# A third Strassen stage in the down projection of a feed-forward block

## Chip, cores and metric

The kernel runs on one core of one Trainium2 chip. The metric is the time of one execution in microseconds (us) as the device reports it; the median of several runs is given. A profiled execution has a time of its own, and its trace has a span, which is a little shorter.

## What is computed

A streaming encoder of two layers on one sequence of 512 tokens, width 1024, in float32. Each layer has a feed-forward block, a mixer (attention and a convolution) and a second feed-forward block:

```python
D_MODEL, SEQ, DEPTH, D_FF = 1024, 512, 2, 2816

def swiglu(x, w_gate, w_up, w_down):
    return (jax.nn.silu(x @ w_gate) * (x @ w_up)) @ w_down

for l in range(DEPTH):
    x = x + 0.5 * swiglu(rms_norm(x, ffn1_norm[l]), ffn1_w_gate[l], ffn1_w_up[l], ffn1_w_down[l])
    ...                                   # mixer: x = x + concat(attn, conv) @ w_out[l]
    x = x + 0.5 * swiglu(rms_norm(x, ffn2_norm[l]), ffn2_w_gate[l], ffn2_w_up[l], ffn2_w_down[l])
    x = rms_norm(x, post_norm[l])
```

So there are four feed-forward blocks. The change concerns their last matrix product, `@ w_down`, from 2816 to 1024.

## The kernel before

**Layout.** Everything is kept transposed: `x` is a tile of 128 partitions x 8 x 512 (8 slices of 128 features, 512 tokens along the free dimension). A product of float32 precision is made of three TensorE matmuls (`mm3`, lines 154 to 156): each operand is split into a high part, a rounded copy made by ScalarE (ACT), and a low part, the rest, made by VectorE (DVE); high x high, high x low and low x high are added in PSUM. Every weight tile therefore costs a load, a cast on ACT (L138 or L244) and a subtraction on DVE (L144 or L246) before TensorE can use it. For some weights the low part is made by a negated copy on ACT (L389) and an accumulating DMA issued by GpSimd (POOL, L390).

**A feed-forward block.** The 2816 hidden features are 22 tiles of 128, in 11 pairs. `CHUNKS` groups the pairs: 0-1, 2-4, 5-7, 8-10. Pairs 0 and 1 use plain products. Pairs 2 to 10 (`pair`) compute gate and up of 256 features with seven products in place of eight (the Strassen-Winograd scheme), from sums of weight quarters that DVE makes (L408 to L411) and from operands that were prepared while pairs 0 and 1 ran. A pair loads its quarters into the buffers `fr` (4 of them) and `raw` (3). Its result is one of two things. `quartered` pairs leave the sums that a Strassen down stage needs (`b11`, `b21`, `b22`, `t1` to `t4`; L445 to L452 and three splits, L161 and L162). The others leave two plain split tiles.

**The down projection.** After pairs 0-1 and after pairs 8-10 it is a *full* one: for each of the 8 slices of the output, `group` runs `mm3` with 512 columns over all hidden tiles of the chunk (4, or 6), then `x` gets its update (L589) and `done(m)` is called. After pairs 2-4 and 5-7 it is a *Strassen stage* (`down`): for each half `g` of the output, seven products of 3 pairs x 2 x 3 matmuls with 256 columns, with sums of weight quarters on DVE (L489, L491, L492, L496) and seven updates of `x` (L480). Both halves' quarters are loaded into the same buffers.

**What follows a block.** `done(m)` prepares slice `m` of the next block's operand: high part on ACT (L167), low part on DVE (L168), a square on ACT and its sum, on POOL for the first slices and on DVE for the last (L191). In layer 0's second block `done2` does so for two sums. In the last block (`Finish`) the last two slices are computed in halves of the tokens (`halved`, L601), then the result is turned and stored.

**Order.** The program is a straight line of instructions; a planner orders each engine's queue by a simulated time line and places the waits. Some orders are forced with `tc.issue_after`: the products of `pair` and `down` follow each other on TensorE by `order["pe"]`. Within an engine the order is fixed when the program runs. Buffers of one tag are used in rotation: the hi and lo weights have 4 each (`wh`, `wl`), `raw` 3.

Of the kernel before, what the change touches and what calls it, by code (L numbers as in the profile page):

```python
# [18 lines left out]
L = 2  # L19
# [17 lines left out]
WIDE = 6  # L37
NP = 3
NC = 2
CHUNKS = ((0, 2), (2, 5), (5, 8), (8, 11))  # L40
CONV = "DAAD"
AHEAD = 2
PAUSE = 16
# [28 lines left out]


@with_exitstack
def encoder_kernel(ctx: ExitStack, tc: tile.TileContext, xT, consts, vecs, rgain, wgu1, wd1, wdq1,
                   wcv, wql, wkl, wuq, wkv, wout, wgu2, wd2, wdq2, out):
    nc = tc.nc
    PSUM = bass.MemoryType.PSUM
    cpool = ctx.enter_context(tc.tile_pool(name="const", bufs=1))
# [7 lines left out]
    def nm(s):  # L87
        uid[0] += 1
        return f"{s}{uid[0]}"
# [44 lines left out]
    def load_w(src, w, kind=""):  # L134
        raw = wpool.tile([P, WC], FP, tag="raw", name=nm("raw"), bufs=3)
        nc.sync.dma_start(out=raw[:, :w], in_=src)
        hi = wpool.tile([P, WC], FR, tag="wh", name=nm("wh"))
        order["cast"] = A.copy(hi[:, :w], raw[:, :w]).ins  # L138
# [5 lines left out]
        (G if kind in POOLW.split() else V).tensor_tensor(lo[:, :w], raw[:, :w], hi[:, :w].bitcast(FP),  # L144
                                                          ALU.subtract)
        return hi, lo

    def low():
        return wpool.tile([P, WC], FR, tag="wl", name=nm("wl"))
# [96 lines left out]
        order["lo"] = V.tensor_tensor(lo[:, :w], src[:, :w], hi[:, :w].bitcast(FP), ALU.subtract).ins  # L246
        return hi, lo

    def ffn(l, gx, norm, wgu, wd, wdq, gain, done, w0=None, halved=KD):
        with tc.tile_pool(name="f", bufs=4) as fpool:  # L250
            ffn_body(fpool, l, gx, norm, wgu, wd, wdq, gain, done, w0, halved)

    def ffn_body(fpool, l, gx, norm, wgu, wd, wdq, gain, done, w0, halved):

# [203 lines left out]
                     "t3": [w[:, h0] for w in us], "t2": [w[:, h1] for w in us],  # L458
                     "t1": [w[:, h0] for w in vs], "t4": [w[:, h1] for w in vs]}]

        def down(act, chunk):

            n = 2 * NP * P
            for g in range(2):
                a11, a12, a21, a22, s3 = quarters(wdq[l, g, chunk], n)
                px, py, pz = bank(), bank(), bank()

                def times(o, src, name, start, q=None, lo=None):
                    hi, lo = split_into(name, src, n) if q is None else summed(wdq[l, g, chunk, q], src, n, lo)
                    with tc.issue_after(order["pe"]):  # L470
                        for k in range(NP):
                            for i in range(2):
                                c = slice((i * NP + k) * P, (i * NP + k + 1) * P)
                                last = mm3(o[:, i * HS:(i + 1) * HS], hi[:, c], lo[:, c], *act[k][name],
                                           start and k == 0 and i == 0, k == NP - 1, True)
                    order["pe"] = last

                def add(row, h, o, sign):
                    v = x[:, 4 * g + 2 * (1 - row):4 * g + 2 * (1 - row) + 2, h * HS:(h + 1) * HS]
                    return V.scalar_tensor_tensor(v, o.rearrange("p (m t) -> p m t", m=2), 0.5 * sign, v, ALU.mult,  # L480
                                                  ALU.add).ins
                times(px, a11, "b11", True)
                with after("u0"):
                    add(0, 0, px, 1)
                times(py, a12, "b21", True, 1)
                with after("u"):
                    add(0, 0, py, 1)
                with after("first") if g else nullcontext():
                    V.tensor_tensor(s3[:, :n], a11[:, :n], a21[:, :n], ALU.add)  # L489
# [7 lines left out]
                lo = subtracted(wdq[l, g, chunk, 3], a22, n)  # L497
# [23 lines left out]

        for p0, p1 in CHUNKS:
            f0, fn = 2 * p0, 2 * (p1 - p0)
            act = []
            last = p1 == NF // 2
            for p in range(p0, p1):
                if p == 0:
                    os = []
                    for r in range(2):
# [18 lines left out]
                elif p < CHUNKS[0][1]:  # L548
                    for r in range(2):
                        ws = [load_w(wgu[l, p, 2 * r + q], WC) for q in range(2)]  # L550
                        o = [bank(), bank()]
                        if w0 and not r:
                            with tc.issue_after(order["mm"]):
                                plain(o[:1], ws, KS[:KD // 4])
                            with tc.issue_after(order["mm"]):
                                R = norm()
                            with after("spread"):
                                plain(o[:1], ws, KS[KD // 4:])
                                plain([None] + o[1:], ws, range(KD))
# [422 lines left out]
    class Finish:  # L982
# [117 lines left out]
    norm = Norm(st)  # L1100
    for l in range(L):
        nx, st1, done = follow(l, "gm")
        ffn(l, gx, norm, wgu1, wd1, wdq1, vv(l, "g1"), done, w0 if l == 0 else None)
        gx = nx
        nx, st2, done = follow(l, "g2")
        mix(l, gx, Norm(st1), done)
# [4 lines left out]
        if l + 1 < L:  # L1111
# [9 lines left out]
            ffn(l, gx, norm2, wgu2, wd2, wdq2, vv(l, "g2"), done2)  # L1121
            gx = nx

            class NormPost(Norm):
# [21 lines left out]
            norm = NormPost(st3)  # L1146
        else:
            end = Finish(st3, gp)
            ffn(l, gx, norm2, wgu2, wd2, wdq2, vv(l, "g2"), end.done, halved=KD - 2)
            end()  # L1150


# [88 lines left out]
```

## Time and profile before

| | |
|---|---|
| median of 3 runs | 1804.32 us (1804.24 to 1805.02) |
| the profiled execution | 1804.94 us, span 1803.1 us, granted TensorE clock 0.998 |
| TensorE matmul (PE) busy | 1781.6 us, 99% |
| TensorE weight load (PEld) busy | 1603.1 us, 89% |
| VectorE (DVE) busy | 1493.0 us, 83% |
| ScalarE (ACT) busy | 1091.9 us, 61% |
| GpSimd (POOL) busy | 420.2 us, 23% |
| DMA | 226.16 MB, mean 125 GB/s |

Engines work side by side and wait for each other by semaphores. PE's matmuls are pipelined, so a busy PE is not PE at its peak: the distance between the starts of two matmuls says more than their duration. "L589" is line 589 of the kernel. A wait is put down to the instruction that ended last before it.

### The profile page before, as it was taken

Reading aid. Unit: us, or ns where it says so; the run is one execution under the profiler, and the core shown is the slowest. Engines: PE = TensorE matmul, PEld = TensorE weight load, DVE = VectorE, ACT = ScalarE, POOL = GpSimd, SP = SyncE. Lnnn points to the kernel's source line nnn. Section 1 sums busy time; section 2 is a strip of 40 time slices with the busy share of each in tenths; the row PEclk is TensorE's granted clock in tenths of the full one; section 3 lists DMA queues with packets and bytes.
Section 4 is the critical chain, followed back from the end, with each engine's and each line's share of the span. In section 5 each row is a group of like instructions: output and inputs, shape, how many; then the busy total and the mean of one; then the engine's idle time right before and its main releaser. Section 6 shows DMA issues by size and latency. Waiting matters only on the chain. (4 is left out here: it accounts for less than half of the span.)

```text
span 1803.1 us, 29267 instructions
## 1 busy us (share of the span) xinstructions
PE 1781.6 (99%) x11334; PEld 1603.1 (89%) x11334; DVE 1493.0 (83%) x2263; ACT 1091.9 (61%) x1721; POOL 420.2 (23%) x343
## 2 busy tenths in 40 slices
PE   9999999999999999999999999999999999999998
PEld 7899999888788899999888999998978788999997
DVE  7898988689956989898779989876998668989884
ACT  5565656457953575756645656554779435656564
POOL 1000010258943000000310000002689410000102
PEclk9999999999999999999999999999999999999999
DMA  5657574325103466665426575743250125575742
GB/s 167 173 127 182 134 174 125 108 88 136 29 24 100 124 167 160 153 159 129 125 63 169 126 191 122 193 110 111 80 151 3 42 83 161 139 183 134 180 119 74
DMA packets 70412, 226.16 MB, mean 125 GB/s; under 512 B 7936, under 2 KB 8320, under 8 KB 70272
## 3 DMA queue, kind: packets, MB, share of 16 engines
q1 hardware_dynamic: 54000, 169.74, 29.7%
q0 software_dynamic: 16128, 54.53, 17.6%
q8 instruction: 89, 1.46, 0.3%
q14 instruction: 51, 0.42, 0.1%
q10 hardware_dynamic: 144, 0.00, 0.0%
HBM read 222.15 MB, written 2.10 MB: 124 GB/s over the span
## 5 line engine op out<-in xcount | busy, mean ns | idle before, releaser
L155 PE MATMUL ps<-r,wh 128*128 128x256 f32 (+1 forms) x2540 | 805.8, 318 | 0.0
L154 PE MATMUL ps<-r,wh 128*128 128x256 f32 (+1 forms) x2540 | 802.9, 320 | 2.3 <-ACT wh L1060 1.5
L156 PE MATMUL ps<-r,wl 128*128 128x256 f32 (+1 forms) x2348 | 750.0, 321 | 1.7 <-DVE wl L246 1.6
L154 PEld LDWEIGHTS ps<-r,wh 128*128 128x128 f32 x2540 | 480.4, 189 | 44.1 <-ACT wh L138 3.7
L155 PEld LDWEIGHTS ps<-r,wh 128*128 128x128 f32 x2540 | 481.4, 190 | 34.2 <-issue 1.4
L156 PEld LDWEIGHTS ps<-r,wl 128*128 128x128 f32 x2348 | 445.0, 190 | 36.7 <-DVE wl L246 3.2
L373 PE MATMUL ps<-xj,wh 128*128 128x512 f32 x864 | 304.8, 392 | 4.6 <-DVE t L426 4.6
L138 ACT CAST wh<-raw 128x1024 fp32r<-128x1024 f32 (+3 forms) x148 | 132.3, 903 | 203.6 <-PE ps L155 100.3
L390 POOL DMA_DIRECT2D ls<-in_wgu x72 | 62.5, 869 | 734.4 <-ACT ls L389 656.5
L244 ACT CAST wh<-fr 128x1024 fp32r<-128x1024 f32 (+1 forms) x160 | 157.8, 986 | 109.7 <-DVE fr L410 51.3
L144 DVE TENSOR_TENSOR wl<-raw,wh 128x1024 fp32r<-128x1024 f32 (+3 forms) x132 | 145.2, 1108 | 84.7 <-ACT wh L138 84.3
L246 DVE TENSOR_TENSOR wl<-fr,wh 128x1024 fp32r<-128x1024 f32 (+1 forms) x160 | 182.1, 1138 | 20.5 <-ACT wh L244 20.5
L373 PEld LDWEIGHTS ps<-xj,wh 128*128 128x128 f32 x864 | 161.3, 188 | 36.3 <-DVE t L426 6.2
L930 POOL TENSOR_TENSOR y<-y,pr 128x511 f32<-128x511 f32 (+14 forms) x120 | 158.1, 1318 | 54.9 <-ACT pr L926 47.5
L374 PE MATMUL ps<-xj,ls 128*128 128x256 f32 x576 | 161.3, 280 | 0.0
L246 DVE TENSOR_TENSOR wl<-raw,wh 128x1024 fp32r<-128x1024 f32 (+1 forms) x100 | 113.4, 1134 | 14.8 <-ACT wh L244 14.4
L244 ACT CAST wh<-raw 128x1024 fp32r<-128x1024 f32 (+1 forms) x100 | 98.1, 981 | 44.7 <-PE ps L155 27.7
L191 POOL TENSOR_TENSOR r<-r,t 128x512 f32<-128x512 f32 x45 | 75.1, 1678 | 175.7 <-ACT t L187 174.9
L374 PEld LDWEIGHTS ps<-xj,ls 128*128 128x128 f32 x576 | 108.3, 188 | 0.2
L389 ACT ACTIVATE ls<-fr 128x1024 fp32r<-128x1024 f32 (+1 forms) x56 | 56.1, 1001 | 85.3 <-PE ps L374 49.5
L926 ACT ACTIVATE pr<-m,vec 128x511 f32<-128x511 f32 (+14 forms) x120 | 85.8, 737 | 12.4 <-POOL y L930 12.4
L922 DVE SCALAR_TENSOR_TENSOR cv<-m,vec,cv 128x511 f32<-128x511 f32 (+14 forms) x120 | 87.8, 732 | 3.6 <-ACT cv L918 2.2
(242 smaller groups left out, 2926.2 us busy)
## 6 DMA issues: line engine op xcount, KB each, us to landing
fr<-in_wgu SPq DMA_DIRECT2D x112, 512.0 KB, 4.2
ls<-in_wgu POOLq DMA_DIRECT2D x72, 512.0 KB, 6.6
raw<-in_wgu SPq DMA_DIRECT2D x62, 512.0 KB, 4.9
fr<-in_wdq SPq DMA_DIRECT2D x48, 384.0 KB, 5.3
ls<-in_wdq POOLq DMA_DIRECT2D x32, 384.0 KB, 4.7
raw<-in_wd SPq DMA_DIRECT2D x32, 384.0 KB, 3.1
raw<-in_wd SPq DMA_DIRECT2D x32, 256.0 KB, 2.7
raw<-in_wcv SPq DMA_DIRECT2D x16, 512.0 KB, 3.6
```

The costliest lines, as they stand in the source:

```text
L138: order["cast"] = A.copy(hi[:, :w], raw[:, :w]).ins
L144: (G if kind in POOLW.split() else V).tensor_tensor(lo[:, :w], raw[:, :w], hi[:, :w].bitcast(FP), ALU.subtract)
L154: T.matmul(o, lh, rh, start=first, stop=False, skip_group_check=free)
L155: T.matmul(o, lh, rl, start=False, stop=False, skip_group_check=free)
L156: order["mm"] = T.matmul(o, ll, rh, start=False, stop=last, skip_group_check=free).ins
L244: A.copy(hi[:, :w], src[:, :w])
L246: order["lo"] = V.tensor_tensor(lo[:, :w], src[:, :w], hi[:, :w].bitcast(FP), ALU.subtract).ins
L373: T.matmul(o, w[0][:, c], both, start=start and k == 0, stop=False, skip_group_check=True)
L374: last = T.matmul(o[:, 0:HS], w[1][:, c], both[:, 0:HS], start=False, stop=k == 3, skip_group_check=True).ins
L922: V.scalar_tensor_tensor(acc[:, s:], u[c][:, :S - s], tap(k), acc[:, s:], ALU.mult, ALU.add)
L926: A.activation(pr[:, s:], u[c][:, :S - s], AF.Copy, scale=tap(k))
L930: order["conv"] = G.tensor_tensor(acc[:, s:], acc[:, s:], pr[:, s:], ALU.add).ins
```

## The change

Pairs 8 and 9 become quartered pairs in a chunk of their own, and a third Strassen stage with 2 pairs (`NR = 2`) takes their down projection. Pair 10 is left alone in the last chunk: its products are issued ahead of that third stage (`held = pair(p1, False)`), and the full down projection now runs over its two hidden tiles only. The weights of this smaller full projection are loaded for four output slices at a time (`load_cols`, twice) in place of once for each slice. The weights of the third stage come in an array of their own (`wdr`). Two sums of squares move: in `Finish` all of those on whole slices from POOL to DVE, in `done2` the second sum for every other slice.

```diff
-CHUNKS = ((0, 2), (2, 5), (5, 8), (8, 11))
+NR = 2
+CHUNKS = ((0, 2), (2, 5), (5, 8), (8, 10), (10, 11))
...
+    def load_cols(wd, l, m, f0, fn):
+
+        raw = wpool.tile([P, WC], FP, tag="raw", name=nm("raw"), bufs=3)
+        nc.sync.dma_start(out=raw.rearrange("p (m f) -> p m f", m=4),
+                          in_=wd[l, m:m + 4, :, f0 * P:(f0 + fn) * P].rearrange("m p f -> p m f"))
+        hi = wpool.tile([P, WC], FR, tag="wh", name=nm("wh"))
+        A.copy(hi, raw)
+        lo = low()
+        V.tensor_tensor(lo, raw, hi.bitcast(FP), ALU.subtract)
+        return hi, lo
+
+    def part_w(ws, m, fn):
+        return [w[:, m % 4 * fn * P:(m % 4 + 1) * fn * P] for w in ws[m // 4]]
...
-        def down(act, chunk):
+        def down(act, quarters_of):
 
-            n = 2 * NP * P
+            np_ = len(act)
+            n = 2 * np_ * P
             for g in range(2):
-                a11, a12, a21, a22, s3 = quarters(wdq[l, g, chunk], n)
+                a11, a12, a21, a22, s3 = quarters(quarters_of(g), n)
...
-                        for k in range(NP):
+                        for k in range(np_):
...
         for p0, p1 in CHUNKS:
             f0, fn = 2 * p0, 2 * (p1 - p0)
-            act = []
             last = p1 == NF // 2
-            for p in range(p0, p1):
+            act = held if last else []
+            for p in range(p0, p1) if not last else ():
...
                 else:
                     order.setdefault("pe", order["mm"])
-                    act += pair(p, p0 > 0 and not last)
+                    act += pair(p, True)
             if p0 and not last:
-                down(act, (p0 - CHUNKS[0][1]) // NP)
+                c = (p0 - CHUNKS[0][1]) // NP
+                if p1 == CHUNKS[-1][0]:
+                    held = pair(p1, False)
+                down(act, lambda g: wdq[l, g, c] if c < NC else wdr[l, g])
                 continue
...
+            if last:
+                wide_w = [load_cols(wd, l, 4 * q, f0, fn) for q in range(2)]
             for m in range(halved if last else KD):
-                if m in ahead:
+                if last:
+                    pd = bank()
+                    group(pd, part_w(wide_w, m, fn), act, range(fn), fn)
+                elif m in ahead:
...
-                ws = [load_w(wd[l, m, :, f0 * P:(f0 + fn) * P], fn * P) for m in ms]
+                ws = [part_w(wide_w, m, fn) for m in ms]
...
-                self.st.add(x[:, m, :])
+                self.st.add(x[:, m, :], eng=V)
...
-                st4.add(x[:, m, :], last=m == KD - 1)
+                st4.add(x[:, m, :], last=m % 2 == 1)
```

More of the change, by code (lines that the diff above doesn't have):

```diff
@@ L74, in encoder_kernel @@
 @with_exitstack
-def encoder_kernel(ctx: ExitStack, tc: tile.TileContext, xT, consts, vecs, rgain, wgu1, wd1, wdq1,
-                   wcv, wql, wkl, wuq, wkv, wout, wgu2, wd2, wdq2, out):
+def encoder_kernel(ctx: ExitStack, tc: tile.TileContext, xT, consts, vecs, rgain, wgu1, wd1, wdq1, wdr1,
+                   wcv, wql, wkl, wuq, wkv, wout, wgu2, wd2, wdq2, wdr2, out):
     nc = tc.nc
@@ L247, in split_into, with ffn, ffn_body @@
         return hi, lo
-    def ffn(l, gx, norm, wgu, wd, wdq, gain, done, w0=None, halved=KD):
+    def ffn(l, gx, norm, wgu, wd, wdq, wdr, gain, done, w0=None, halved=KD):
         with tc.tile_pool(name="f", bufs=4) as fpool:
-            ffn_body(fpool, l, gx, norm, wgu, wd, wdq, gain, done, w0, halved)
-    def ffn_body(fpool, l, gx, norm, wgu, wd, wdq, gain, done, w0, halved):
+            ffn_body(fpool, l, gx, norm, wgu, wd, wdq, wdr, gain, done, w0, halved)
+    def ffn_body(fpool, l, gx, norm, wgu, wd, wdq, wdr, gain, done, w0, halved):
         def quarter():
@@ L459, in pair @@
                      "t1": [w[:, h0] for w in vs], "t4": [w[:, h1] for w in vs]}]
-        def down(act, chunk):
-            n = 2 * NP * P
+        def down(act, quarters_of):
+            np_ = len(act)
+            n = 2 * np_ * P
             for g in range(2):
-                a11, a12, a21, a22, s3 = quarters(wdq[l, g, chunk], n)
+                a11, a12, a21, a22, s3 = quarters(quarters_of(g), n)
                 px, py, pz = bank(), bank(), bank()
                 def times(o, src, name, start, q=None, lo=None):
-                    hi, lo = split_into(name, src, n) if q is None else summed(wdq[l, g, chunk, q], src, n, lo)
+                    hi, lo = split_into(name, src, n) if q is None else summed(quarters_of(g)[q], src, n, lo)
                     with tc.issue_after(order["pe"]):
-                        for k in range(NP):
+                        for k in range(np_):
                             for i in range(2):
-                                c = slice((i * NP + k) * P, (i * NP + k + 1) * P)
+                                c = slice((i * np_ + k) * P, (i * np_ + k + 1) * P)
                                 last = mm3(o[:, i * HS:(i + 1) * HS], hi[:, c], lo[:, c], *act[k][name],
-                                           start and k == 0 and i == 0, k == NP - 1, True)
+                                           start and k == 0 and i == 0, k == np_ - 1, True)
                     order["pe"] = last
@@ L1102, in encoder_kernel @@
         nx, st1, done = follow(l, "gm")
-        ffn(l, gx, norm, wgu1, wd1, wdq1, vv(l, "g1"), done, w0 if l == 0 else None)
+        ffn(l, gx, norm, wgu1, wd1, wdq1, wdr1, vv(l, "g1"), done, w0 if l == 0 else None)
         gx = nx
@@ L1148, in encoder_kernel @@
             end = Finish(st3, gp)
-            ffn(l, gx, norm2, wgu2, wd2, wdq2, vv(l, "g2"), end.done, halved=KD - 2)
+            ffn(l, gx, norm2, wgu2, wd2, wdq2, wdr2, vv(l, "g2"), end.done, halved=KD - 2)
             end()
@@ L1175, in quarters, with down_quarters, down_main, down_rest @@
         return w.transpose(1, 5, 6, 3, 4, 0, 2, 7).reshape(L, NF // 2, 4, P, WC)
-    def down_quarters(w):
-        n0, n1 = CHUNKS[0][1], CHUNKS[-1][0]
-        w = w.reshape(L, NF // 2, 2, P, 2, 2, 2, P)[:, n0:n1, :, :, :, ::-1].reshape(L, NC, NP, 2, P, 2, 2, 2, P)
-        return w.transpose(0, 5, 1, 6, 3, 4, 7, 2, 8).reshape(L, 2, NC, 4, P, 2 * NP * P)
+    def down_quarters(w, n0, nc, np_):
+        w = w.reshape(L, NF // 2, 2, P, 2, 2, 2, P)[:, n0:n0 + nc * np_, :, :, :, ::-1]
+        w = w.reshape(L, nc, np_, 2, P, 2, 2, 2, P)
+        return w.transpose(0, 5, 1, 6, 3, 4, 7, 2, 8).reshape(L, 2, nc, 4, P, 2 * np_ * P)
+    def down_main(w):
+        return down_quarters(w, CHUNKS[0][1], NC, NP)
+    def down_rest(w):
+        return down_quarters(w, CHUNKS[-2][0], 1, NR)[:, :, 0]
     def feat(v):
@@ L1229 @@
         "wgu2": quarters(a["ffn2_w_gate"], a["ffn2_w_up"]), "wd2": cols(a["ffn2_w_down"]),
-        "wdq2": down_quarters(a["ffn2_w_down"]),
+        "wdq2": down_main(a["ffn2_w_down"]), "wdr2": down_rest(a["ffn2_w_down"]),
     }
```

6 lines of the change are left out of this document (3 added, 3 removed).

## The prediction

> **What bounds the kernel now.** I read the page first, then the windows of the feed-forward block that runs from 0 to 350 us, then who waits for whom, then the groups of instructions by shape. The page's first row gives the engines' busy times:
>
> ```profile
> PE 1781.6 (99%) x11334; PEld 1603.1 (89%) x11334; DVE 1493.0 (83%) x2263; ACT 1091.9 (61%) x1721; POOL 420.2 (23%) x343
> ```
>
> TensorE has nearly no hole, so time can only leave if its own work shrinks, and it returns wherever another engine makes it wait. DVE at 83% is an average, so I asked for stretches (columns after the length: PE, PEld, DVE, ACT and POOL busy, granted clock, DMA share, GB/s).
>
> ```profile
> 228.00:246.00 18.00, 18.00 (x152) 17.97 (x151) 16.50 (x26) 8.68 (x13) 1.72 (x2) 1.00 0.62 157
> 330.00:348.00 18.00, 18.00 (x81) 14.89 (x80) 18.00 (x20) 12.88 (x20) 8.02 (x5) 1.00 0.53 168
> 200.00:220.00 20.00, 20.00 (x147) 18.94 (x146) 19.15 (x32) 13.62 (x20) 1.73 (x2) 1.00 0.60 140
> 166.30:257.30 91.00, 90.13 (x686) 86.71 (x685) 82.20 (x126) 57.40 (x81) 8.55 (x11) 1.00 0.63 156
> 257.30:349.60 92.30, 92.30 (x580) 83.61 (x579) 71.86 (x99) 54.40 (x79) 12.94 (x11) 1.00 0.49 127
> 328.70:349.60 20.90, 20.90 (x94) 17.28 (x93) 20.06 (x22) 14.54 (x22) 9.27 (x6) 1.00 0.47 150
> 353.00:360.00 7.00, 7.00 (x32) 5.81 (x31) 0.00 (x0) 0.42 (x1) 0.00 (x0) 1.00 0.17 66
> 876.70:897.70 21.00, 21.00 (x94) 17.41 (x93) 20.44 (x21) 19.75 (x31) 11.74 (x7) 1.00 0.50 149
> 1770.40:1792.60 22.20, 22.20 (x138) 20.02 (x138) 10.17 (x17) 12.63 (x21) 8.44 (x6) 1.00 0.06 18
> ```
>
> The first is inside a Strassen down stage: nothing but 256-column matmuls, 152 touched, each edge cutting one or two, so 18.00 / 150.5 = 0.120 us from start to start. The second is inside the full down projection, 512 columns each: 18.00 / 79.5 = 0.226 us. A matmul half as wide costs 53%, not 50%. The fourth is one steady period (a down stage and three quartered pairs): DVE is busy 82.2 of 91.0. The fifth is the part that changes (pairs 8 to 10 and the full down): DVE busy 71.9 of 92.3, 20.4 idle. The third shows that DVE at 19.15 of 20 still let TensorE run without a hole; the sixth, that the last 20.9 us of the block already hold 20.06 us of DVE work; the seventh, that DVE then rests for at least 7 us in the next block's first products.
>
> Who waits, over the whole program (engine, line, releaser: us in total, times, longest):
>
> ```profile
> PEld ps L373 <- DVE t L426: 6.2, 8, 0.8
> PEld ps L156 <- DVE wl L246: 3.2, 7, 0.5
> ACT ls L389 <- DMA fr<-in_wdq: 13.5, 7, 2.0
> DVE raw L489 <- DMA fr<-in_wdq: 6.5, 7, 1.1
> ```
>
> There are eight Strassen down stages (two in each of four blocks), and both waits of TensorE's weight loads come about once in each: just before it, where the third pair's outputs are drained late, and inside it, where a weight's low part is late. 9.4 / 8 = 1.2 us a stage.
>
> **TensorE's term.** Pairs 8 and 9 lose their full down: 4 tiles of F x 8 outputs x 3 matmuls = 96 of 512 columns, 96 x 0.226 = 21.70 us. The third stage adds 2 halves x 7 products x 2 pairs x 2 x 3 = 168 of 256 columns, 168 x 0.120 = 20.16 us. Saved: 1.54 us a block. In the last block two of the eight outputs are done in halves: before 108 x 0.226 + 72 x 0.120 = 33.05, after 36 x 0.226 + 24 x 0.120 = 11.02 and 20.16, saved 1.87. Over four blocks 3 x 1.54 + 1.87 = 6.5 us, which is 0.36%: one multiplication in eight is saved, but most of it is paid back in the dearer narrow matmul. In the first window PEld is full (17.97 of 18), in the second it is not (14.89): every 256 columns now bring a weight load.
>
> [...]
>
> **DVE's term.** The rows by shape (mean ns), and five rows of the timeline that show how instructions overlap:
>
> ```profile
> L480 DVE SCALAR_TENSOR_TENSOR x<-ps,x 128x512 f32<-128x512 f32 x112 | 76.7, 685 | 6.4 <-PE ps L156 6.4
> L162 DVE TENSOR_TENSOR r<-t,r 128x512 fp32r<-128x512 f32 x96 | 65.1, 683 | 4.7 <-ACT r L161 4.7
> L144 DVE TENSOR_TENSOR wl<-raw,wh 128x768 fp32r<-128x768 f32 x38 | 42.3, 1122 | 19.3 <-ACT wh L138 19.3
> L144 DVE TENSOR_TENSOR wl<-raw,wh 128x1024 fp32r<-128x1024 f32 x56 | 75.1, 1344 | 61.0 <-ACT wh L138 60.6
> L168 DVE SCALAR_TENSOR_TENSOR r<-x,vec,r 128x512 fp32r<-128x512 f32 x32 | 41.3, 1300 | 3.4 <-ACT r L167 3.4
> L168 DVE SCALAR_TENSOR_TENSOR r<-x,first_gain,r 128x512 fp32r<-128x512 f32 x8 | 5.6, 750 | 3.0 <-ACT r L167 3.0
> L191 POOL TENSOR_TENSOR r<-r,t 128x512 f32<-128x512 f32 x45 | 75.1, 1678 | 175.7 <-ACT t L187 174.9
> L191 DVE TENSOR_TENSOR r<-r,t 128x512 f32<-128x512 f32 x19 | 14.2, 750 | 4.5 <-POOL r L191 3.7
> L138 ACT CAST wh<-raw 128x768 fp32r<-128x768 f32 x38 | 31.5, 829 | 47.2 <-issue 23.8 <-PE ps L155 17.8 <-PE ps L373 5.5
> L138 ACT CAST wh<-raw 128x1024 fp32r<-128x1024 f32 x72 | 76.6, 1075 | 130.5 <-PE ps L155 77.5 <-issue 48.4 <-DMA raw<-in_wgu 3.9
> ```
>
> ```profile
> 228.15 0.42 DVE L449 TENSOR_TENSOR u<-t,t 128x256 f32<-128x256 f32 x1
> 228.49 0.68 DVE L162 TENSOR_TENSOR r<-t,r 128x512 fp32r<-128x512 f32 x1
> 229.09 0.42 DVE L451 TENSOR_TENSOR t<-t 128x256 f32<-128x256 f32 x1
> 229.43 0.42 DVE L450 TENSOR_TENSOR u<-u,t 128x256 f32<-128x256 f32 x1
> 229.77 0.68 DVE L480 SCALAR_TENSOR_TENSOR x<-ps,x 128x512 f32<-128x512 f32 x1
> ```
>
> Starts lie 0.34 us (256 columns) and 0.60 us (512) apart: an instruction occupies DVE for its duration less 0.08. In each half the third stage has 4 weight sums, 5 low parts and 7 updates of x, all 512 wide: 16 x 0.60 x 2 = 19.2 us. Quartered outputs of pairs 8 and 9: three splits of 512 and five pieces of 256 in place of two splits, 3 x 0.60 + 5 x 0.34 - 2 x 0.60 = 2.3 each, 4.6. Eight low parts of 768 go and two of 1024 come: -8 x 1.04 + 2 x 1.26 = -5.8. In all +18.0 us. So DVE has 71.9 + 18.0 = 89.9 us of work in a stretch that TensorE alone would finish in 92.3 - 1.5 = 90.8. The idle 20 us are used up.
>
> Most of that is bearable: the steady stage shows 96% without a hole. The third stage itself asks 19.2 of 20.2 us (95%). Pair 10, not quartered, lets DVE catch up ahead of it. I charge this stage the two known waits. From below they cost nothing (pair 10 gives slack), from above the 1.2 us of the rows; its sums are 512 wide instead of 768, so I take two thirds, 0.8 us x 4 = 3.2 us.
>
> **The hand-over at the block's end.** Before, an output row took 18 matmuls, 4.07 us; after, 6, 1.36 us. All eight are through in 8 x 1.36 = 10.9 us. Each still asks DVE for the x update (0.60) and the low part of the next block's operand (L168), and ACT for its high part and squares; POOL adds the squares. L168 takes 1300 ns in such places and 750 ns on the kernel's first input, where the squares are added on DVE: here POOL's adds of 1678 ns run beside it. [...]
>
> The next block's first two groups take products 0 to 6 first, 3 x 0.226 = 0.68 us each, so operand 6 is due 10.9 + 6 x 0.68 = 15.0 us after the full down starts; nothing else stands in TensorE's queue behind it that could run. In the window 328.70 to 349.60 two kinds of weights stand between DVE's updates, the full down's own and the next block's:
>
> ```profile
> L144 DVE TENSOR_TENSOR wl<-raw,wh 128x768 fp32r<-128x768 f32 x4 | 4.2, 1074 | 0.0
> L144 DVE TENSOR_TENSOR wl<-raw,wh 128x1024 fp32r<-128x1024 f32 x3 | 4.1, 1378 | 0.0
> ```
>
> DVE spent 20.06 us there from the first x update to past operand 6. The four 768-wide low parts go (4.2), one 1024-wide comes (1.3): 17.2, and 1.4 for the first row's products: ready at 18.6, 3.6 us late. From below nothing is late, if the three next-block weights (4.1 us) come earlier or later. I take about the middle, 2 us, for the two blocks that hand over to the mixer. For layer 0's second block ACT decides: 19.75 us in its window (876.70 on), less 3.3 of casts, plus 1.1, is 17.5, and 1.4 before and 1.2 of DVE after: 20.1, 5.1 late at most; I take 3. Together 7 us, between 0 and 12.3.
>
> The last block ends the program. From its first x update DVE has 10.17 - 4.2 + 1.3 + 5 adds x 0.67 (now its own) = 10.6 us to do while TensorE now has 11.0 - 1.4 = 9.6: 1.0 us late at most, none if the wide weights come earlier; I take the 1.0, since ACT (12.63 - 3.3 + 1.1 = 10.4) is as late.
>
> Loads: on SP's queue wide_w needs two in place of eight, and the third stage brings eight quarters; POOL's queue gets four more accumulating ones. POOL is busy 8.6 and ACT 57.4 of 91.0 us in the steady period, and I cost them at nothing. What covers them is the time between a buffer's release and its next product; if that is gone, the second rival decides.
>
> **Sum.** -6.5 + 3.2 + 7 + 1 = +4.7 us. The profiled execution took 1804.94 us, 1.84 of it outside the span of 1803.1, and stands 0.6 above the median: 1809.6 there, 1809.0 in the median.
>
> **Rivals.** *The hand-over is hidden* (faster). DVE's 7 idle us after 353 show that what trails may trail further, and the planner may place the next block's weights elsewhere. It holds if operand 6 is ready within 15.0 us. Then -6.5 + 3.2 = -3.3, or -6.5 with the waits gone too: 1797.8 to 1801.0. Against it: 20.06 busy of 20.9.
>
> *The third stage's second half waits for its loads* (slower still). Its third and fourth quarters are loaded into buffers that the first half frees, and already now ACT and DVE wait 2.0 and 1.1 us for them in seven of eight stages. A product there takes 18 x 0.120 = 2.16 us, in the third stage 1.44, so of seven products' cover 5 us go. The loads are a third smaller, and 256-column work of the first half leaves some slack; if 2.5 us a block come through, 10 us are added: 1819.
>
> *It partly cancels*: hand-overs at 0.5 us to 1 us each: 1802 to 1806. That it doesn't do what it says is hardly open: the wait chains of the third stage are those of the first two.
>
> **Numbers.** The hand-over case (1806 to 1812) has 0.40, the loads 0.13, the hidden hand-over 0.27, cancelling 0.20. 0.2% is 3.6 us, about what a measurement of this kernel tells from no change; the bounds are 1800.7 and 1807.9. The hidden case lies mostly below 1800.7 (0.22), cancelling and the edges of both neighbours within (0.28), the rest above (0.50). The range 1798 to 1818 leaves out one in ten on each side.
>
> **What would show it.** In the changed profile: 168 more 256-column and 96 fewer 512-column matmuls a block; L480 x168; DVE over 95% from pair 8 to the block's end; TensorE's weight loads waiting for L168 at the start of the next block. I am wrong if these waits are missing (then it is faster), or if they stand at L246 or L389 inside the third stage.

## The result

The changed kernel takes 1817.11 us (median of four runs, 1816.28 to 1817.88) against 1804.28 (1804.02 to 1805.02) for the kernel before in the same comparison. The ratio is 1.0070, 95% interval 1.0054 to 1.0086: slower by 12.8 us, or 8 us more than the forecast's 4.7. The profiled execution took 1816.28 us, its span is 1814.5, 11.4 more than before.

The code above `down` grew, so lines shift: L154 to L156 are now L169 to L171, L168 is L183, L191 is L206, the sums of squares that TensorE makes are L213 (L198 before), L138 and L144 are L139 and L145, L246 is L261, L373, L389 and L426 are L388, L404 and L441, L480 is L496, L489 to L496 are L505 to L512, L589 is L613. The experiments' kernels shift some lines once more; where a row needs it, the text says so.

The page's row of busy times, and the row of the Strassen stages' updates of `x` (line, engine, operation, tiles, shape, count, busy, mean ns, idle before):

```profile
PE 1781.6 (98%) x11598; PEld 1614.4 (89%) x11598; DVE 1573.8 (87%) x2423; ACT 1123.5 (62%) x1785; POOL 418.3 (23%) x351
L496 DVE SCALAR_TENSOR_TENSOR x<-ps,x 128x512 f32<-128x512 f32 x168 | 115.5, 688 | 10.3 <-PE ps L171 8.7
```

The counts are those foreseen: 264 matmuls more, 168 updates in place of 112. TensorE is busy for as long as before and 98% in place of 99% of a longer span; DVE has 80.8 us more to do. So look at who waits (engine, line, releaser: us in total, times, longest):

```profile
PEld ps L213 <- DVE r L206: 9.3, 2, 8.7
PEld ps L388 <- DVE t L441: 7.3, 12, 0.8
PEld ps L171 <- DVE wl L261: 6.8, 8, 1.4
PEld ps L170 <- DVE r L183: 2.4, 2, 1.4
ACT ls L404 <- DMA fr<-in_wdq: 8.0, 4, 2.7
```

One wait outweighs the rest: 8.7 us in which TensorE waits at L213 for the chain of sums of squares (L206), once, at 908.8 us, where layer 0's second block hands over to layer 1. The others are the forecast's: the drained products ahead of a stage (L388), a weight's low part inside a stage (L261, 3.2 us before, now with four of 1.4 us, one in each third stage), and the next block's operand (L183, 0.3 us before), twice, at the two mixers.

The windows around that hand-over, first of the kernel before, then of the changed one (length, then PE, PEld, DVE, ACT and POOL busy, granted clock, DMA share, GB/s):

```profile
876.70:908.20 31.50, 31.50 (x141) 26.08 (x140) 27.15 (x27) 27.00 (x42) 20.67 (x12) 1.00 0.42 130
897.70:908.20 10.50, 10.50 (x49) 8.67 (x48) 6.71 (x7) 7.25 (x12) 8.93 (x6) 1.00 0.26 91
908.20:1030.60 122.40, 121.54 (x721) 107.19 (x720) 109.50 (x177) 68.34 (x102) 9.95 (x10) 1.00 0.48 125
```

```profile
889.50:917.50 28.00, 19.71 (x94) 16.23 (x92) 26.29 (x28) 24.22 (x37) 15.21 (x9) 0.89 0.35 115
909.00:917.50 8.50, 0.21 (x2) 0.04 (x1) 7.28 (x5) 6.67 (x11) 7.79 (x5) 0.64 0.29 93
917.50:921.00 3.50, 3.50 (x17) 3.50 (x17) 0.84 (x3) 0.00 (x0) 1.04 (x1) 0.50 0.00 0
921.00:925.00 4.00, 4.00 (x11) 3.13 (x11) 1.79 (x5) 0.00 (x0) 1.01 (x1) 0.50 0.00 0
917.50:1043.40 125.90, 125.13 (x720) 110.27 (x721) 107.79 (x175) 67.40 (x101) 9.00 (x10) 0.97 0.45 115
```

The first row of each runs from the full down's first update of `x` to the first sums at L213. The chain between them took 31.5 us and takes 28.0; it hardly got shorter. But TensorE had 31.50 us of products to run meanwhile, and now has some 19.3. It waits for the difference, 8.7 us, while DVE, POOL and ACT are 78 to 92% busy. Then the granted clock is 0.50 for 7.5 us, and the stretch from the sums to the first Strassen update of the next block takes 125.9 us where it took 122.4 (908.2 to 1030.6). So this one hand-over costs 8.5 + 3.5 = 12.0 us, as much as the whole loss.

Measured in the same way, from the last update of the second Strassen stage to the next block's sums, the blocks before the two mixers take 0.4 and 0.2 us longer than before, and the last block, to the end of the program, 0.7. There the saving of TensorE and the new waits come out even. (The four make some 13.2; over the rest of the program the profiled execution is 1.8 us shorter.)

### The profile page after: what moved, and what is told of

It is laid out like the page before. It is cut to its first block, busy times and chain, and to the rows that moved or that the text cites. A ratio compares the mean times of both kernels' runs of the same rounds, so it can differ in the third digit from the quotient of the medians.

```text
span 1814.5 us, 30169 instructions
## 1 busy us (share of the span) xinstructions
PE 1781.6 (98%) x11598; PEld 1614.4 (89%) x11598; DVE 1573.8 (87%) x2423; ACT 1123.5 (62%) x1785; POOL 418.3 (23%) x351
## 5 line engine op out<-in xcount | busy, mean ns | idle before, releaser
L170 PE MATMUL ps<-r,wh 128*128 128x256 f32 (+1 forms) x2628 | 819.8, 312 | 1.6 <-DVE r L183 1.6
L169 PE MATMUL ps<-r,wh 128*128 128x256 f32 (+1 forms) x2628 | 816.5, 314 | 1.1 <-ACT wh L139 0.5
L171 PE MATMUL ps<-r,wl 128*128 128x256 f32 (+1 forms) x2372 | 743.4, 316 | 5.2 <-DVE wl L261 5.1
L169 PEld LDWEIGHTS ps<-r,wh 128*128 128x128 f32 x2628 | 498.3, 190 | 38.7 <-ACT wh L139 3.1
L170 PEld LDWEIGHTS ps<-r,wh 128*128 128x128 f32 x2628 | 499.4, 190 | 31.5 <-DVE r L183 2.4
L171 PEld LDWEIGHTS ps<-r,wl 128*128 128x128 f32 x2372 | 450.5, 190 | 35.8 <-DVE wl L261 6.8
L388 PE MATMUL ps<-xj,wh 128*128 128x512 f32 x864 | 304.7, 393 | 4.9 <-DVE t L441 4.6
L259 ACT CAST wh<-fr 128x1024 fp32r<-128x1024 f32 (+2 forms) x184 | 172.6, 938 | 130.4 <-DVE fr L425 51.4
L261 DVE TENSOR_TENSOR wl<-fr,wh 128x1024 fp32r<-128x1024 f32 (+2 forms) x184 | 199.3, 1083 | 15.3 <-ACT wh L259 15.3
L139 ACT CAST wh<-raw 128x1024 fp32r<-128x1024 f32 (+4 forms) x116 | 105.2, 917 | 151.6 <-PE ps L170 94.2
L388 PEld LDWEIGHTS ps<-xj,wh 128*128 128x128 f32 x864 | 160.8, 188 | 36.9 <-DVE t L441 7.3
L145 DVE TENSOR_TENSOR wl<-raw,wh 128x1024 fp32r<-128x1024 f32 (+4 forms) x100 | 116.4, 1171 | 56.5 <-ACT wh L139 56.1
L389 PE MATMUL ps<-xj,ls 128*128 128x256 f32 x576 | 161.3, 280 | 0.0
L259 ACT CAST wh<-raw 128x1024 fp32r<-128x1024 f32 (+2 forms) x116 | 108.0, 931 | 55.7 <-PE ps L170 31.5
L261 DVE TENSOR_TENSOR wl<-raw,wh 128x1024 fp32r<-128x1024 f32 (+2 forms) x116 | 124.9, 1076 | 15.7 <-ACT wh L259 14.9
L496 DVE SCALAR_TENSOR_TENSOR x<-ps,x 128x512 f32<-128x512 f32 x168 | 115.5, 688 | 10.3 <-PE ps L171 8.7
L404 ACT ACTIVATE ls<-fr 128x1024 fp32r<-128x1024 f32 (+2 forms) x64 | 61.1, 955 | 87.6 <-PE ps L389 49.6
L389 PEld LDWEIGHTS ps<-xj,ls 128*128 128x128 f32 x576 | 108.3, 188 | 0.0
```

What stands on the lines that cost most here:

```text
L169: T.matmul(o, lh, rh, start=first, stop=False, skip_group_check=free)
L170: T.matmul(o, lh, rl, start=False, stop=False, skip_group_check=free)
L171: order["mm"] = T.matmul(o, ll, rh, start=False, stop=last, skip_group_check=free).ins
L259: A.copy(hi[:, :w], src[:, :w])
L388: T.matmul(o, w[0][:, c], both, start=start and k == 0, stop=False, skip_group_check=True)
L389: last = T.matmul(o[:, 0:HS], w[1][:, c], both[:, 0:HS], start=False, stop=k == 3, skip_group_check=True).ins
```

## The experiments

All are timed beside the kernel before on the same chip. The theories: **A**, the loss is the chain of sums at layer 0's second block; its rival **B**, it is spread over the four third stages. Below them: what makes that chain long, what makes the holes in the third stages (**C**), and what makes those at the mixers (**D**: by **D1** POOL's additions, 1.3 to 2.0 us each there, make DVE's low parts late; by **D2** DVE is full).

**1. The late norm.** The norm of the layer's output is applied later in the next block, as the kernel does already in its first block: the sums at L213 stand behind the gate product and half the up product of the first pair's second tile instead of ahead of them. Core of the edit:

```diff
+            norm.postponed = True
...
-                            if not w0:
-                                R = norm()
-                    if not w0:
+                            R = norm()
+                    if not postponed:
                         scaled(os, R)
```

> The changed kernel, but in layer 1's first block TensorE asks for the sums of squares half a product group later (8.1 us of matmuls more ahead of them) and for the spread norm among pair 1's products, as the first block of the program does. Theory A (the loss sits at the hand-over of layer 0's second block: TensorE waits 8.3 us for the sums of squares, then runs at half clock): the wait is at most 1 us, the clock stays at 1.00 and the time falls by 11 to 12 us to 1805 to 1806. Rival B (VectorE is overloaded in every block's third stage and the loss is spread): the wait comes back elsewhere in the same block, 1813 or more.

Measured: 1808.38 us, ratio 1.0024 (1.0014 to 1.0034). TensorE comes to the sums at 916.7 us, waits 0.77, and the clock stays:

```profile
909.00:918.00 9.00, 8.62 (x41) 6.90 (x39) 7.49 (x5) 6.17 (x9) 7.10 (x5) 1.00 0.28 87
917.50:921.00 3.50, 3.50 (x24) 3.20 (x25) 1.18 (x5) 0.00 (x0) 1.44 (x2) 1.00 0.10 38
```

Two thirds of the loss go with one wait: A, though some 3 us of the promise are missing. The four holes in the third stages are still 1.42 us each, and those at the mixers 1.46 and 1.59. Part of what is missing stands in the trace: from the last update of layer 0's second block's second Strassen stage (806.79) to the first of the next block (1033.04) it takes 226.2 us, 1.9 more than in the kernel before (806.26 to 1030.56). The profiled execution is also the shortest of the nine (1806.65 to 1812.52), so the trace is not that of a typical one. The late norm wasn't run in the kernel before, so what it costs by itself isn't known.

**2. All of that chain's additions on DVE.**

```diff
-                st3.add(x[:, m, :], last=m == KD - 1)
+                st3.add(x[:, m, :], eng=V)
...
-                st4.add(x[:, m, :], last=m % 2 == 1)
+                st4.add(x[:, m, :], eng=V)
```

> The changed kernel with all sums of squares of layer 0's second block on VectorE, none on GpSimd. Theory A1 (the chain is long because GpSimd's adds of 1.3 to 2.3 us and VectorE's own instructions hold each other up): the adds take 0.7 us, the wait for the sums falls from 8.3 to about 3 us and the time to 1809 to 1811. Rival A2 (ScalarE's 32 passes over the slices, 18 us, set the chain's length, or VectorE has no time for nine more adds): the wait stays above 7 us and the time at 1816 or more.

Measured: 1815.72 us, ratio 1.0066 (1.0054 to 1.0078).

```profile
PEld ps L213 <- DVE r L206: 7.0, 2, 6.5
909.20:915.80 6.60, 0.51 (x4) 0.09 (x2) 6.06 (x8) 6.44 (x11) 0.00 (x0) 0.70 0.40 119
```

The wait falls by 2.2 us only, to 6.5, between what A1 and A2 expected and nearer to A2. With POOL out of it, ACT is busy for 6.44 of the 6.60 us that TensorE waits, 1.0 of it for a cast of the next weights: here its passes over the slices set the length of the chain. In the changed kernel itself POOL is the fuller of the two (7.79 of 8.50 us, ACT 6.67), so there both carry the chain; taking POOL's additions away uncovers ACT's passes.

**3. The third stage's weight quarters loaded for both halves at once** (the same bytes in half as many transfers, none of them in the second half; the accumulating loads that make two of the low parts stay in each half):

```diff
+                both = quarters(lambda q: both_halves[:, q].rearrange("g p n -> p g n"), 2 * n, split=2)
...
+                    a11, a12, a21, a22, s3 = (v[:, g * n:(g + 1) * n] for v in both)
```

> The changed kernel, but the third stage's weight quarters of both halves are loaded together (512 KB each) ahead of the first half, so that the second half waits for no load. Rival of the prediction (the second half is late because its loads wait for freed buffers): the hole of 1.4 us at the third product of the second half, once in each block, is gone: 5 us less, 1812. Theory C (VectorE works there without a pause and has the instructions in a bad order): the hole stays, 1816 to 1818.

Measured: 1818.85 us, ratio 1.0080 (1.0067 to 1.0093). All four holes stay at 1.42 us, and the wait for the sums is 9.9. The rival of the prediction by which the second half waits for its quarters' loads falls.

**4. The third stage left out of layer 0's second block**, which is done as before; the other three have it. **5. The reverse**: it alone has it. The core of both is one condition on the chunks; the full down projection and the sums of squares of the blocks without a third stage go back with it:

```diff
+OLD = ((0, 2), (2, 5), (5, 8), (8, 11))
...
-        for p0, p1 in CHUNKS:
+        old = l == 0 and wd is wd2            # 5: not (l == 0 and wd is wd2)
+        for p0, p1 in OLD if old else CHUNKS:
```

> The third stage in three of the four blocks; layer 0's second block has its chunks, its down projection and its sums of squares as before the change. Theory A: 1804.5 to 1806, since the other three blocks lose what they gain. Rival B (a like loss in each block): three quarters of 12.8 us remain, 1813 to 1815.

> The third stage in layer 0's second block alone, the other three blocks as before. Theory A (nearly all of the loss is this block's hand-over to the next layer: 8.5 us of wait and 3.5 of slow clock behind it, less the 1.5 that the block's products save and with 1.3 for its hole): some 1804.2 + 12 = 1816, between 1815 and 1817. Rival B (the loss is spread over the four blocks, some 3 us each): 1807 to 1808.

Measured: without that block 1806.77 us, ratio 1.0015 (1.0007 to 1.0024); that block alone 1815.21 us against 1803.1, ratio 1.0069 (1.0055 to 1.0083), its wait at the sums 8.7 us. 12.1 us of the loss are in this block and 2.7 in the other three (together 14.8, the whole change 12.8, within what the intervals allow). The first is a little over A's 1806 and far from B's 1813, the second is where A has it. A is shown from both sides.

**6. The low part first.** Where does the hole in the third stage come from? DVE's queue in the second half, in the changed kernel:

```profile
326.62 0.68 DVE L507 TENSOR_TENSOR fr<-fr,fr 128x512 f32<-128x512 f32 x1
327.21 0.69 DVE L496 SCALAR_TENSOR_TENSOR x<-ps,x 128x512 f32<-128x512 f32 x1
327.81 0.68 DVE L508 TENSOR_TENSOR fr<-fr,fr 128x512 f32<-128x512 f32 x1
328.51 0.69 DVE L496 SCALAR_TENSOR_TENSOR x<-ps,x 128x512 f32<-128x512 f32 x1
329.12 0.68 DVE L512 TENSOR_TENSOR raw<-raw,fr 128x512 f32<-128x512 f32 x1
329.93 0.69 DVE L496 SCALAR_TENSOR_TENSOR x<-ps,x 128x512 f32<-128x512 f32 x1
330.53 0.68 DVE L261 TENSOR_TENSOR wl<-fr,wh 128x512 fp32r<-128x512 f32 x1
```

TensorE stands from 329.85 until L261 at 330.53, which needs only L508 and ACT's cast of it (L259, done at 329.21), but comes behind the sum of the quarter `a12` (L512) and an update. That order looks like the fault, so in the second half the update from `py` was put behind L261 and L512 behind the update of a later product:

```diff
                 times(px, a11, "t2", False)
+                if late_rest:
+                    with after("lo"):
+                        add(0, 0, py, 1)
...
+                if late_rest:
+                    with after("third"):
+                        V.tensor_tensor(a12[:, :n], a12[:, :n], a11[:, :n], ALU.add)
```

> In the second half of each third stage the two updates of the third accumulator's forerunner (py) and the sum of a12 come behind the low part of the third product's operand on DVE, nothing else is changed. Theory C1 (the hole of 1.43 us in TensorE's issue at the third product is DVE's order: the low part, L261, stands behind updates and a sum that nobody waits for yet): the four holes shrink from 1.43 us to 0.3 or less and the time falls by 4 to 5 us, to some 1812.5. Rival C2 (DVE has no room in the third stage in any order): the hole moves to the next product of the same half and is as long, and the time stays within 1.5 us of 1817. The wait of 8.7 us ahead of the sums of layer 0's second block stays by both, and may grow by what TensorE comes earlier there (1.3 us), which would give 1813 to 1814.

Measured: 1824.71 us, ratio 1.0124 (1.0110 to 1.0138): slower again, by more than either theory had.

```profile
PEld ps L170 <- DVE r L183: 14.0, 14, 2.7
PEld ps L171 <- DVE wl L261: 2.0, 5, 0.5
```

The four holes went (L261 6.8 to 2.0 us), so it was DVE's order that made them. But at the hand-overs the operand's low parts (L183) now make TensorE's weight loads wait 14.0 us in 14 places, 2.4 in 2 before. The expectation's C2, by which DVE has no room in any order, isn't shown by that: between the stage's third product and the hand-over DVE is busy for 9.27 of 12.00 us only (`in_wcv` are weights of the mixer):

```profile
330.00:342.00 12.00, 12.00 (x78) 10.96 (x77) 9.27 (x13) 4.28 (x5) 0.00 (x0) 1.00 0.57 180
341.30 1.05 ACT L139 CAST wh<-raw 128x1024 fp32r<-128x1024 f32 x1 [1.99 <-DMA raw<-in_wcv]
342.38 1.23 DVE L145 TENSOR_TENSOR wl<-raw,wh 128x1024 fp32r<-128x1024 f32 x1 [1.21 <-ACT wh L139]
```

DVE waits here for a cast that waits for its load, and the next update of `x` and the low parts of the operand stand behind it in its queue; in the other two blocks that hand over to a next one DVE waits for such casts twice, 1.07 to 1.26 us each. So the edit exchanged one bad order for another. Why the loads came when they did wasn't tested.

**7. A fifth of the third stage's DVE work taken away** (three of 16 instructions in each half). The kernel leaves out the three sums of quarters that are made in place, so the output is another one; TensorE's products stay:

```diff
+                    if np_ != NR:
+                        V.tensor_tensor(a21[:, :n], a21[:, :n], a22[:, :n], ALU.add)
+                        V.tensor_tensor(a11[:, :n], a11[:, :n], a21[:, :n], ALU.add)
...
+                    if np_ != NR:
+                        V.tensor_tensor(a12[:, :n], a12[:, :n], a11[:, :n], ALU.add)
```

> The changed kernel, and in the third stage the three sums of weight quarters that are made in place (a21 + a22, a11 + a21, a12 + a11) are left out in both halves, so that the numbers that come out are other ones: 24 sums of 0.6 us, 14 us of DVE's time, TensorE's products the same. Theory C2 (DVE has no room from pair 8 to the end of the block, and the holes are its queue): the four holes of 1.43 us go, those at the mixers (1.34 and 1.0) shrink to under 0.3, and the time falls by 6 to 8 us, to 1809 to 1811; the wait ahead of the sums of layer 0's second block stays at 8.5 us or grows by the 1.3. Rival C3 (a fixed wait of the products' order: ACT's high parts or the banks of sums): the holes stay and the time falls by less than 2 us.

Measured: 1812.41 us, ratio 1.0050 (1.0038 to 1.0063); span 1809.4, 5.1 less than the changed kernel's.

```profile
PEld ps L213 <- DVE r L206: 8.7, 1, 8.7
PEld ps L170 <- DVE r L183: 2.8, 3, 1.2
PEld ps L171 <- DVE wl L261: 1.9, 5, 0.5
```

The holes go, and the span falls by what they cost: 4 x 1.3 us. The sums left out also stand ahead of the late operand (ACT's cast waits for L508), so this run alone doesn't tell a full queue from a long chain; with experiment 6, where the holes went with the sums in place, it is DVE's queue. C2 expected more, 1809 to 1811, and was wrong on the mixers: 1.2 and 1.0 us stay there (L183), so those holes aren't the third stage's backlog. And the wait at the sums stays at 8.7, since its chain starts when the products end and moves with them.

**8. The additions ahead of the mixers on DVE instead of POOL**, in the changed kernel, with the three blocks of experiment 4, with the late norm, and in the kernel before:

```diff
-            st.add(x[:, m, :], last=m == KD - 1)
+            st.add(x[:, m, :], last=m == KD - 1, eng=V if name == "gm" else None)
```

> The adds of squares of the block ahead of each mixer are made by DVE alone instead of by POOL; all else as in the changed kernel. [...] Rival D2 (DVE is full from pair 8 to the end of the block, and each add laid on it makes the low parts later still): the holes grow to 2 us or more and the time rises by 1 to 3 us, to 1818 to 1820.

> Third stage in three of the four blocks (layer 0's second block as before), and the adds of squares ahead of each mixer on DVE instead of POOL. The same three blocks without the second edit took 2.7 us more than the kernel before, and the second edit by itself took the holes at the mixers out of TensorE's issue (1.34 and 1.0 us) and 0.9 us off the time. Theory E1 (what is left of the loss there is the mixers' hand-over, and the two add up): 1804 to 1805, no difference from the kernel before. Rival E2 (each mixer's hand-over gives back in another place what the adds on DVE gain): 1806.5 to 1807.

> Third stage in all four blocks, the norm of layer 0's second block applied late, the adds ahead of the mixers on DVE. Theory E1: 1808.4 less 1 to 1.9, 1806.5 to 1807.5. Rival E2: 1808.4 again. With the low part first in the third stage's second half as well, 1810.9 was measured: if that edit alone costs what it cost by itself (7.6), this one comes to 1804 or less.

> The kernel before, with the adds of squares ahead of the mixers on DVE and nothing else: it tells whether what the runs above gain by these adds belongs to the third stage. If the third stage's shorter hand-over made POOL's adds late (D1): within 1 us of the kernel before. If they are late without it too: 1 to 2 us less than the kernel before, and the two runs above are to be set against this one.

Measured: 1815.07 us, ratio 1.0066 (1.0053 to 1.0079) in the changed kernel; 1804.65, 1.0002 (0.9993 to 1.0011) with the three blocks; 1807.45, 1.0024 (1.0015 to 1.0032) with the late norm; 1803.79, 0.9998 (0.9990 to 1.0007) in the kernel before. The wait at the mixers in the changed kernel with this edit:

```profile
PEld ps L170 <- DVE r L183: 0.5, 1, 0.5
```

So DVE's additions do cure it: both holes are gone, although DVE has more to do there. D1 holds. The timeline ahead of the first mixer shows why (start, duration), first in the changed kernel, then with the edit:

```profile
350.50 1.98 POOL L206 TENSOR_TENSOR r<-r,t 128x512 f32<-128x512 f32 x1 [0.26 <-ACT t L202]
351.25 1.78 DVE L183 SCALAR_TENSOR_TENSOR r<-x,vec,r 128x512 fp32r<-128x512 f32 x1
...
354.50 1.29 POOL L206 TENSOR_TENSOR r<-r,t 128x512 f32<-128x512 f32 x1 [2.02 <-ACT t L202]
354.81 2.06 DVE L145 TENSOR_TENSOR wl<-raw,wh 128x1024 fp32r<-128x1024 f32 x1
356.80 1.40 DVE L183 SCALAR_TENSOR_TENSOR r<-x,vec,r 128x512 fp32r<-128x512 f32 x2
357.59 0.50 PE L170 MATMUL ps<-r,wh 128*128 128x512 f32 x1 [0.95 <-DVE r L183]
```

```profile
350.83 0.75 DVE L183 SCALAR_TENSOR_TENSOR r<-x,vec,r 128x512 fp32r<-128x512 f32 x1
...
352.09 1.22 DVE L145 TENSOR_TENSOR wl<-raw,wh 128x1024 fp32r<-128x1024 f32 x1
```

Beside POOL's additions the same DVE instructions take 1.78 and 2.06 us in place of 0.75 and 1.22; the cause of that was not tested. What the edit is worth in time is at the edge of what the runs resolve: nothing to 1 us in the changed kernel, 2.3 us (by the ratios, 0.0013) with three blocks, and by the ratio nothing with the late norm. With three blocks this is the best version with a third stage, and it is no faster than the kernel before.

**9. Late norm, low part first and the mixers' additions on DVE together.**

> Three edits to the changed kernel at once: the norm of the mixer's output after layer 0's second block is applied behind the first products of the next block, as in the run with the late norm; the low part first in the second half of each third stage; the adds ahead of the mixers on DVE. If the three causes (late sums 8.7 us, holes in the third stage 4 times 1.3, hand-overs to the mixers 1.9) are separate: 1808.4 less 5 less 1.5, that is 1801 to 1803, under the kernel before. If DVE has no room in any order (C2, D2): 1808 to 1811, no better than the late norm by itself.

Measured: 1810.87 us, ratio 1.0046 (1.0033 to 1.0058), 0.0022 above the same kernel without the low part first. The causes aren't separate: with the low part first each mixer has two holes again (1.08 and 1.00 us, 1.18 and 1.02), though POOL's additions are gone there, and TensorE waits 3.5 us for the sums, in the late place too.

## Why the prediction was right in sign and short in size

**TensorE's term** (-6.5 us) held. Inside the third stage the windows show nothing but 256-column matmuls without a hole, 97 touched and 95 started in 11.30 us, 0.119 us from start to start (0.120 foreseen), with the weight loads full and DVE at 99%:

```profile
318.50:329.80 11.30, 11.30 (x97) 11.30 (x96) 11.18 (x19) 6.23 (x12) 1.72 (x2) 1.00 0.67 148
258.20:349.00 90.80, 89.61 (x640) 84.34 (x639) 82.22 (x129) 59.36 (x90) 11.53 (x12) 1.00 0.56 136
258.20:360.50 102.30, 100.16 (x687) 92.75 (x685) 92.69 (x140) 64.05 (x97) 16.04 (x14) 1.00 0.53 134
```

At 0.119 us, 168 matmuls take 20.0 us, and the 21.7 of the 96 wide ones less that is 1.7, near the forecast's 1.54 us a block.

**DVE's term** (+18.0 us a block) held too: 92.69 us from the second stage's end to the sums, where the kernel before has 74.00 in 258.30 to 360.20, +18.7. The sign named for it didn't: I said over 95% from pair 8 to the block's end, and it is 82.22 of 90.80, 91%, because pair 10 leaves DVE some rest and 10 us of its work trail into the next block.

**The third stage's waits** (0.8 us each, bound 1.2) measured 1.3 each (1.43 between two starts, less 0.12), 5.2 for 3.2. What failed there is scaling the old stages' wait by the instructions' width; experiments 6 and 7 show that it is DVE's queue, full to 99% there, so that a low part comes late by the instructions queued ahead of it. I had written that a wait at L246 inside the third stage would prove me wrong; it stands there, and the runs put it down to DVE (6, 7), not to the quarters' loads (3).

**The mixers' hand-overs** (2 + 2 us) cost 1.1 and 0.8 (holes of 1.34 and 1.00 between two starts, less the usual 0.226), at the operand, L183, as foreseen; experiment 8 shows that POOL's additions beside it make it late, and experiment 7 that less DVE work ahead of it hardly helps; I had summed the count of DVE's instructions.

**Layer 0's second block** (3 us, at most 5.1) made the block 12.0 us longer. This is the step that failed. "ACT decides" was half of it: ACT is full through the wait once POOL's additions are gone (experiment 2), and beside them POOL is fuller still. But I summed ACT's work in a window that ended with the last update of `x`, at 897.7, and set it against operand 6. TensorE waits there for the sums of squares, which come behind that operand, and the row of 897.70 to 908.20 shows the part left out: 7.25 us of ACT and 8.93 of POOL, under 10.50 us of products that hid them. Nothing in the list of waits of the kernel before named this chain, since it ended just as TensorE came for it. The second part, 3.5 us at half clock behind the wait, had no term.

**The last block's end** (+1.0): its stretch is 0.7 us longer, with 1.87 saved and a hole of 1.3, so the end cost 1.2. That this fits is luck. In the changed kernel's trace the granted clock is 0.50 from 1805.8 to 1809.1, under the last products, where the kernel before still ran at 1.00. In the four traces with the same last block and the full clock there (experiment 1, the three blocks of 4, and both with the mixers' additions on DVE) the stretch takes 102.8 to 102.9 us, against 103.05 in the kernel before and 103.7 in the changed one, so by them the end itself costs some 0.4 us.

By blocks, forecast and measured: +1.3 and +0.4; +2.3 and 12.0; +1.3 and +0.2; -0.1 and +0.7. Three of four blocks nearly break even, in part because their errors cancel: the third stages' waits came out dearer than forecast and the mixers' hand-overs cheaper. The three-block runs say the same: 4.95 saved, 3.9 in holes, 0.4 to 1.2 at the end, and a ratio of 1.0002 measured once the mixers' holes are gone. So the sign of the whole was decided by the one term that was mis-sized, and that the forecast had the right sign is luck in part. What remains open is the rest of the missing 3 us of experiment 1. Putting the low part first cost some 9 us by the times, each set against the kernel before, and 8.0 by the spans; the waits of TensorE's weight loads grew by some 7, and its trace has more half clock, 3.4 us in a mixer (459.3 to 462.7) among it.

## What to carry to other kernels

When work is taken from the bounding engine ahead of a hand-over, take from the trace the whole chain from its first producer to the first instruction that waits for it, and set that against the bounding engine's work left beside it; a chain that ends exactly when it is needed shows as no wait at all, as the 31.5 us ahead of L213 did in the kernel before. A trade of one engine's time for another's wants room on the second in that stage: here, at 99%, a low part came 1.3 us late behind its queue, and a new order brought TensorE's waits for such parts (L261) from 6.8 to 2.0 us and those at the hand-overs (L183) from 2.4 to 14.0. And first see whether the consumer can be asked for later, which here recovered 8 us with one norm moved.

## What the runs showed of the hardware

Whether the granted clock fell at a hole in TensorE's work, when, and for how long, can be read off five of these waits (a hole is counted from the start of the last matmul ahead of it to the start of the next). After one of 2.64 us (at a mixer, experiment 6) the clock stayed at 1.00. In one of 6.5 us (experiment 2) it was at 0.50 from 2.5 us after the hole's beginning, in one of 8.7 us (the changed kernel) from 2.7, in one of 9.9 us (experiment 3) from 5.0. After one of 3.46 us (experiment 9) it fell 1.5 us after TensorE had gone on. Rows of experiment 6, the changed kernel, experiments 2, 3 and 9, and the kernel before:

```profile
357.30:363.00 5.70, 5.70 (x29) 4.88 (x30) 2.90 (x7) 0.00 (x0) 0.32 (x1) 1.00 0.19 76
```

```profile
908.80:911.40 2.60, 0.38 (x2) 0.00 (x0) 2.54 (x2) 2.51 (x5) 2.60 (x2) 1.00 0.00 0
911.50:925.10 13.60, 7.63 (x26) 6.76 (x27) 7.47 (x11) 4.26 (x7) 7.33 (x6) 0.50 0.18 58
```

```profile
909.30:911.75 2.45, 0.38 (x2) 0.00 (x0) 2.45 (x4) 2.45 (x4) 0.00 (x0) 1.00 0.16 20
911.80:922.00 10.20, 6.23 (x23) 5.65 (x24) 5.94 (x13) 4.37 (x7) 2.04 (x2) 0.50 0.22 73
```

```profile
909.10:914.05 4.95, 0.38 (x2) 0.00 (x0) 4.95 (x3) 4.73 (x9) 4.87 (x4) 1.00 0.16 49
914.10:927.70 13.60, 8.73 (x29) 7.57 (x30) 6.38 (x11) 2.28 (x4) 6.23 (x5) 0.50 0.11 39
```

```profile
914.60:919.50 4.90, 1.83 (x16) 1.48 (x14) 4.13 (x5) 0.68 (x2) 1.82 (x2) 1.00 0.50 156
919.60:922.95 3.35, 3.35 (x11) 2.77 (x11) 1.23 (x5) 0.00 (x0) 1.80 (x2) 0.50 0.01 2
```

```profile
1400.90:1404.25 3.35, 3.28 (x6) 1.97 (x7) 1.85 (x3) 2.31 (x4) 0.02 (x1) 0.50 0.00 0
```

So the length of the hole alone doesn't decide, and the last row shows half clock without a long hole: from 1385 to 1410 no two matmul starts are over 1.3 us apart. The half clock lasts 3.4, 10.2 or 13.65 us, which is one, three or four times 3.41 (13.65 / 4). With the same wait of 8.7 us it lasts 13.65 us in the changed kernel and 10.2 us in experiment 5, so what a hole costs beyond itself isn't fixed by its length.

The way back to 1.00, from the first matmul behind the hole, took 4.9 us (experiment 9) to 8.8 us (experiment 3), and 7.6 in the changed kernel (917.47 to 925.11). There and in experiment 3 the first 3.4 us of these go to the 16 sums of one column (L213); whether that made the way back longer wasn't tested.
